# A pooling and mLSTM block on one core: the pooling mixer's group matrices folded into the input projection's weights, the gate applied there too

## The chip, the cores and the metric

The kernel runs on one core of a Trainium2 chip. The metric is device time in microseconds (us) from launch to end; 2048 tokens of 1024 channels go through the block once. Engines are named as in the profile: PE (TensorE), DVE (VectorE), ACT (ScalarE), POOL (GpSimd), and SP (SyncE), which here only issues transfers.

## The reference, cut to what matters

All columns come from one input projection. Branch A pools the u columns over time, multiplies each group of 256 channels by a 256 x 256 matrix, scales each channel and gates it:

```python
h = rms_norm(x, norm_pre_g)
proj = jnp.einsum('bsd,de->bse', h, w_in)              # 1024 -> 9232 columns
u_a, z_a, q, k, v, o, z_b, gates, g_a, g_b = jnp.split(proj, split_points, axis=-1)

pooled = multiscale_pool(u_a)          # group g: mean over a centred window of 2/4/8/16 tokens, minus the token
mixed = jnp.einsum('bsgc,gcd->bsgd', pooled.reshape(B, S, 4, 256), pool_mix_w).reshape(B, S, 1024)
y_a = (mixed * pool_scale) * jax.nn.silu(z_a)
...                                    # branch B: bidirectional mLSTM on q, k, v and the gates -> y_b
p_a = jnp.einsum('bsc,cd->bsd', y_a, w_proj_pool)
p_b = jnp.einsum('bsc,cd->bsd', y_b, w_proj_mlstm)
merged = jax.nn.sigmoid(g_a + b_merge[0]) * p_a + jax.nn.sigmoid(g_b + b_merge[1]) * p_b
out = x + rms_norm(jnp.einsum('bsd,de->bse', merged, w_out), norm_post_g)
```

Pooling acts along the tokens and the group matrix along the channels, so the two commute: pooling `h @ (w_u @ (mix * scale))` gives the same numbers as mixing and scaling the pooled `h @ w_u`.

## The kernel before, in words

**Precision.** A float32 matrix product is done as three products of rounded halves: each operand is split into `hi` (rounded to fp32r, a copy on ACT) and `lo` (the remainder, a subtraction on DVE or POOL; `split`, lines 91 to 98), and PE multiplies hi·hi, hi·lo and lo·hi (`mm3`, lines 106 to 108, with 512 columns; `acc3`, lines 920 to 922, with 256).

**Input projection** (`phase1`). The tokens are taken in two halves of 1024. In each, the columns go by in 36 pairs of 128 + 128 (`in_pairs` writes their order): q, k, v, u, z, o, ga and gb of four heads or groups. A pair is computed by Strassen's scheme in its Winograd form (`strassen`): seven products of 12 matmuls, named by operand (A11·B11, S2·T2, S1·T1, S3·T3, A12·B21, A22·T4, S4·B22), into PSUM banks A, B and C (two buffers each). Bank B is read three times: by the addition to `u2`, by that to `u3` (L395, L400) and at the end. On PE the products of two neighbouring pairs interleave: A11·B11 and S2·T2 of pair i, A22·T4 and S4·B22 of pair i-1, then S1·T1, S3·T3 and A12·B21 of pair i.

In half 0 a pair's weights are loaded (`load_w`, 512 KB at a time), differenced on DVE (L352), split, and the four combinations T1 to T4 kept in memory (`wt{i}`); half 1 loads these back (`again_w`). Columns u are gathered in `raw` and pooled in `pair_u`: doubling sums of windows (the first on POOL, the rest on DVE, L684), the mean minus the token (L688), the few tokens at the edges (L692, L693), then a transfer to `pooled{g}` in memory. Columns z become their SiLU and go to `zs{g}` (`pair_z`). Group g's u pair is number 12, 14, 22, 25 in the order, its z pair 6, 13, 19, 26.

**After it** come the mLSTM (chunks of 128 tokens), branch A, branch B and the output projection, with PE going from one to the next without a barrier. Branch A works on token tiles of 256 (`TT`). For each tile, `mixer` loads the four groups' pooled columns and gates (`xz`), splits the pooled ones (`pxs`), multiplies them by the group's matrix in 48 matmuls (`mps`), scales and gates (L1024), and splits the result (`pys`). `branch_a` multiplies that by w_proj_pool in 192 matmuls per tile (`paps`) and by the sigmoid of g_a. The weights of w_proj_pool are split into 16 blocks (8 row blocks, two column halves): two in `aside` during the mLSTM, four in `then` towards its end, ten once the mLSTM's buffers are free.

**Order.** A scheduler sets each engine's order from the program's order, priorities and its own estimate of times. `tc.issue_after(x)` keeps what is issued within it behind instruction x. Transfers are issued by SP in one list, in order. Pools of a few buffers tie steps together: `acc` (4), `raw` (3) and `p` (6) for the columns, `wraw` (3) and `wc` (20) for weights, `tr` (2) in PSUM for transposes.

Of the kernel before, what the change touches and what calls it, by code (L numbers as in the profile page):

```python
# [13 lines left out]
P = 128  # L14
S = 2048
# [22 lines left out]
LAP = 1  # L38
PB = 2
# [3 lines left out]
PX = "kT"  # L43
# [4 lines left out]
def in_pairs():  # L48
# [11 lines left out]
    light = [("v", 0), ("o", 0), ("z", 0), ("o", 1), ("v", 1), ("o", 2), ("z", 1), ("o", 3), ("v", 2), ("o", 4)]  # L60
    light += [("z", 2), ("o", 5), ("v", 3), ("o", 6), ("z", 3), ("o", 7)]
# [16 lines left out]
class Kernel:  # L78
# [21 lines left out]
    def mm3(self, ps, w, x, start, stop):  # L100

        nc = self.nc
        for kt in range(4):
# [4 lines left out]
            nc.tensor.matmul(ps, wl, xh, start=False, stop=stop and kt == 3, skip_group_check=True)  # L108
# [195 lines left out]
    def load_w(self, wr, i, kts):  # L304
        raw = wr.tile([P, 4, 2 * P], F32, tag="wraw", name=self.nm("wraw"))
        self.nc.sync.dma_start(raw, self.a["w_in"][i, :, kts, :])
        return raw

    def again_w(self, W, i, wr, wc):

        nc, w_in = self.nc, self.a["w_in"]
# [9 lines left out]
        nc.sync.dma_start(left, w_in[i, :, :, :P])  # L321
# [11 lines left out]
        self.read = nc.sync.dma_start(b22, w_in[i, :, 4:8, P:])  # L333
# [35 lines left out]
    def strassen(self, H, W, psum, pool, out, n=BLK, swap=False):  # L369
# [13 lines left out]
        def prod(k, h, w, start):  # L383
            x, y = (H[h], W[w]) if not swap else (W[w], H[h])
            self.mm3(bank[k], y, x, start, True)
# [12 lines left out]
        prod("B", "S3", "T3", False)  # L398
# [38 lines left out]
    def phase1(self):  # L437
        tc, nc, a = self.tc, self.nc, self.a
        with ExitStack() as es:
# [22 lines left out]
            for half in range(2):  # L462
# [49 lines left out]
                rest = iter(())  # L512
                for i in range(2, n):
# [146 lines left out]
    def pair_u(self, half, kind, g, H, W, psum, pool):  # L660
# [6 lines left out]
        for i in range(2):  # L667
# [26 lines left out]
            nc.sync.dma_start(self.sp[f"pooled{g}"][:, i, tstart : tstart + n], d[:, :n])  # L694
# [66 lines left out]
    def spills(self):  # L761
# [4 lines left out]
        for h in range(NH):  # L766
# [4 lines left out]
            for k in ("pooled", "zs", "sga", "sgb"):  # L771
                sp[f"{k}{h}"] = self.dram(f"{k}{h}", [P, 2, S])
# [136 lines left out]
    def late_constants(self):  # L909
        self.cpool = self.ctx.enter_context(self.tc.tile_pool(name="const2", bufs=1, reuse_waits="tile"))  # L910
        self.pscale = self.load("pool_scale", [P, KT])
# [58 lines left out]
    def mix_weights(self, raws, pool):  # L970
        nc = self.nc
        out = []
        for g in range(4):
            raw = raws.tile([P, 2, DH], F32, tag="wraw", name=self.nm("mraw"))
            nc.sync.dma_start(raw, self.a["pool_mix_w"][g])
            out.append(tuple(pool.tile([P, 2, DH], F32R, tag="w", name=self.nm(f"mx{p}")) for p in "hl"))
            self.split(*out[g], raw, "act", "dve")
        return out

# [23 lines left out]
    def mixer(self, t, mix, ya):  # L1003
        nc, sp = self.nc, self.sp
        cut = slice(t * TT, (t + 1) * TT)
        for g in range(4):
            xz = self.pair_of("kT", "xz", F32)
            nc.sync.dma_start(xz[:, 0], sp[f"pooled{g}"][:, :, cut])
            nc.sync.dma_start(xz[:, 1], sp[f"zs{g}"][:, :, cut])
            z = xz[:, 1]  # L1010
            xs = self.pair_of(PX, "pxs")
            self.split(xs[:, 0], xs[:, 1], xz[:, 0], "act", "dve")
            ys = ya[t, g] = self.pair_of("v1h" if g < 2 else "v1l", "pys")
            for i in range(2):
                ps = self.psum.tile([P, 512], F32, tag="t", name=self.nm("mps"), bufs=PB)[:, :TT]
                self.acc3(
                    ps,
                    [
                        (tuple(w[:, kt, i * P : (i + 1) * P] for w in mix[g]), (xs[:, 0, kt, :], xs[:, 1, kt, :]))
                        for kt in range(2)  # L1020
                    ],
                )
                ct = 2 * g + i
                nc.vector.scalar_tensor_tensor(  # L1024
                    z[:, i, :], ps, self.pscale[:, ct : ct + 1], z[:, i, :], op0=ALU.mult, op1=ALU.mult
                )
# [545 lines left out]
```

## Time and profile before

| | |
|---|---|
| median of 3 runs | 2386.11 us (2384.36 to 2393.65) |
| the profiled execution | 2388.18 us, its span 2386.4 us, granted clock 0.993 |
| instructions on PE, DVE, ACT, POOL | 12569, 2495, 1773, 902 |
| half 0, half 1 of the projection | up to 730 us, up to 1440 us |
| mLSTM, branch A, branch B, output | up to 1790.5, 2031.5, 2215 and 2386.4 us |
| matmuls of the mixer (`mps`) | 384 |
| transferred | 521.63 MB, mean 219 GB/s |

The span runs from the first to the last instruction; the execution's own time has little around it. The stages were cut where PE goes from one kind of matmul to the next; neighbours overlap by a few us. A row of the profile that groups instructions gives line, engine, operation, output<-inputs (numbers left out), shape and count; then busy time and mean ns of one; then the idle time before them and what ended it. PE's busy time counts the latency of overlapping matmuls once. A row of a stage gives its bounds and length, the busy time (and instructions) of PE, PEld (weight loads), DVE, ACT and POOL, the granted clock, the DMA engines' busy share, and GB/s.

### The profile page before, as it was taken

The page shows a single profiled execution, that of the slowest core. Times are in us where ns is not written, and L with a number is a line of the kernel's source. Part 1 is how long each engine was busy: PE and PEld are TensorE (multiplying, and loading weights), DVE is VectorE, ACT ScalarE, POOL GpSimd, SP SyncE. Part 2 cuts the span into 40 slices and gives each one's busy share as a digit, 9 for nine tenths or more (in the row PEclk, how much of TensorE's full clock was granted, in tenths as well). Part 3 has the DMA queues.
Part 4 walks back from the last instruction along what each step waited for, and adds up shares of the span by engine and source line. Part 5 has one row for each costly group of instructions (what it writes and reads, how often), then busy time and mean ns, then how long its engine had stood idle before and what let it go on. Part 6 is the DMA issues. An engine that isn't in the chain of part 4 may idle for free.

```text
span 2386.4 us, 35771 instructions
## 1 busy us (share of the span) xinstructions
PE 2313.3 (97%) x12569; PEld 1998.1 (84%) x12569; DVE 1468.2 (62%) x2495; ACT 898.2 (38%) x1773; POOL 1139.3 (48%) x902
## 2 busy tenths in 40 slices
PE   7899999999999989999999999998999999999998
PEld 5688888888887878888888887997989899999776
DVE  6876676677666465565666434887875333354765
ACT  5435333333334333323322234766764112120442
POOL 4655564555544434464564540554555111233775
PEclk9999999999999999999999999999999999999999
DMA  4467656566673566787787867766657546588763
GB/s 151 175 225 273 234 194 238 203 230 215 233 260 135 166 192 216 260 282 256 246 272 239 269 221 253 231 214 208 197 161 230 176 146 208 183 283 280 249 215 124
DMA packets 303011, 521.63 MB, mean 219 GB/s; under 512 B 27504, under 2 KB 138224, under 8 KB 302832
## 3 DMA queue, kind: packets, MB, share of 16 engines
q1 hardware_dynamic: 302832, 519.35, 65.3%
q8 instruction: 99, 1.62, 0.3%
q14 instruction: 80, 0.66, 0.1%
HBM read 318.45 MB, written 200.80 MB: 218 GB/s over the span
## 4 chain that ended last, share of the span: by engine, by line
PE 79%; DVE 8%; DMA 7%; issue 2%; POOL 2%; ACT 2%; SPq 1%; DVEq 0%; POOLq 0%; ACTq 0%
PE bankB L106 8%; PE bankB L107 8%; PE bankB L108 8%; PE bankA L108 5%; PE bankA L107 5%; PE bankC L107 5%; PE bankA L106 5%; PE bankC L106 5%; PE bankC L108 5%; PE num L1212 3%; PE pb L921 2%; PE pb L922 2%; PE pb L920 2%; PE paps L921 2%; PE paps L922 2%
## 5 line engine op out<-in xcount | busy, mean ns | idle before, releaser
L98 POOL TENSOR_TENSOR wB21l<-wraw,wB21h 128x512 fp32r<-128x512 f32 x76 | 107.6, 1416 | 218.9 <-ACT wB21h L94 178.8
L627 DVE SCALAR_TENSOR_TENSOR acc<-raw,conv_w,acc 128x1026 f32<-128x1026 f32 (+1 forms) x96 | 155.8, 1636 | 10.6 <-ACT acc L622 9.7
L1196 POOL TENSOR_TENSOR qs<-q,isc 128x256 f32<-128x256 f32 x120 | 91.6, 766 | 145.3 <-PE num L1212 63.4
L98 POOL TENSOR_TENSOR wB22l<-wraw,wB22h 128x512 fp32r<-128x512 f32 x76 | 116.6, 1535 | 77.8 <-ACT wB22h L94 55.8
L922 PE MATMUL pb<-oxs,w_proj_mlstml 128*128 128x256 f32 x512 | 143.8, 281 | 0.0
L921 PE MATMUL pb<-oxs,w_proj_mlstmh 128*128 128x256 f32 x512 | 143.8, 281 | 0.0
L920 PE MATMUL pb<-oxs,w_proj_mlstmh 128*128 128x256 f32 x512 | 143.5, 280 | 0.0
L921 PE MATMUL paps<-pys,w_proj_poolh 128*128 128x256 f32 x512 | 142.6, 281 | 0.2 <-POOL pys L98 0.2
L920 PE MATMUL paps<-pys,w_proj_poolh 128*128 128x256 f32 x512 | 141.6, 281 | 1.2 <-DVE sga L1049 1.2
L922 PE MATMUL paps<-pys,w_proj_pooll 128*128 128x256 f32 x512 | 141.3, 281 | 0.0
L98 POOL TENSOR_TENSOR wB11l<-wraw,wB11h 128x512 fp32r<-128x512 f32 x72 | 108.9, 1513 | 54.4 <-ACT wB11h L94 53.6
L395 DVE TENSOR_TENSOR u<-bankB,p 128x512 f32<-128x512 f32 x76 | 52.2, 687 | 107.8 <-PE bankB L108 95.1
L106 PE MATMUL bankC<-S1h,wT1h 128*128 128x512 f32 x272 | 106.5, 392 | 3.4 <-ACT sg L738 3.4
L106 PE MATMUL bankB<-S3h,wT3h 128*128 128x512 f32 x272 | 106.3, 391 | 2.3 <-DVE u L395 2.3
L108 PE MATMUL bankB<-S2h,wT2l 128*128 128x512 f32 x272 | 106.3, 391 | 1.2 <-DVE wT2l L98 1.2
L106 PE MATMUL bankA<-A12h,wB21h 128*128 128x512 f32 x272 | 106.8, 393 | 0.5 <-ACT p L389 0.5
L107 PE MATMUL bankB<-S2l,wT2h 128*128 128x512 f32 x272 | 107.0, 393 | 0.0
L106 PE MATMUL bankB<-A22h,wT4h 128*128 128x512 f32 x272 | 105.9, 389 | 0.8 <-DVE u L400 0.8
L108 PE MATMUL bankC<-S1h,wT1l 128*128 128x512 f32 x272 | 106.5, 392 | 0.0
L107 PE MATMUL bankC<-S1l,wT1h 128*128 128x512 f32 x272 | 106.4, 391 | 0.0
L106 PE MATMUL bankB<-S2h,wT2h 128*128 128x512 f32 x272 | 106.2, 391 | 0.0
L107 PE MATMUL bankB<-S3l,wT3h 128*128 128x512 f32 x272 | 106.0, 390 | 0.0
(443 smaller groups left out, 7677.9 us busy)
## 6 DMA issues: line engine op xcount, KB each, us to landing
wraw<-in_w_in SPq DMA_DIRECT2D x110, 512.0 KB, 4.4
wt<-wT2h SPq DMA_DIRECT2D x34, 256.0 KB, 3.8
wt<-wT1h SPq DMA_DIRECT2D x34, 256.0 KB, 4.6
wt<-wT3h SPq DMA_DIRECT2D x34, 256.0 KB, 3.8
wt<-wT2l SPq DMA_DIRECT2D x34, 256.0 KB, 4.8
wt<-wT1l SPq DMA_DIRECT2D x34, 256.0 KB, 4.3
wt<-wT3l SPq DMA_DIRECT2D x34, 256.0 KB, 3.1
wt<-wT4h SPq DMA_DIRECT2D x34, 256.0 KB, 2.0
```

The costliest lines, as they stand in the source:

```text
L98: return eng.tensor_tensor(lo, x, hi.bitcast(F32), op=ALU.subtract)
L106: nc.tensor.matmul(ps, wh, xh, start=start and kt == 0, stop=False, skip_group_check=True)
L107: nc.tensor.matmul(ps, wh, xl, start=False, stop=False, skip_group_check=True)
L108: nc.tensor.matmul(ps, wl, xh, start=False, stop=stop and kt == 3, skip_group_check=True)
L395: self.read_banks.append(nc.vector.tensor_tensor(u2, bank["B"], p1, op=ALU.add))
L627: nc.vector.scalar_tensor_tensor(acc[:, :n], raw[:, tap : tap + n], self.cw[:, ct, tap : tap + 1], acc[:, :n], op0=ALU.mult, op1=ALU.add,)
L920: nc.tensor.matmul(ps, wh, xh, start=i == 0, stop=False)
L921: nc.tensor.matmul(ps, wh, xl, start=False, stop=False)
L922: nc.tensor.matmul(ps, wl, xh, start=False, stop=i == n)
L1196: nc.gpsimd.tensor_tensor(qs[d], q[:, :, ck], isc[:, d, j % 2, None, :].to_broadcast([P, 2, P]), op=ALU.mult)
L1212: nc.tensor.matmul(pn, qs[d][:, kt, :], state[:, kt, :], start=kt == 0, stop=False)
```

## The change

The mixer's matmuls leave the tail. For each group the matrix `pool_mix_w[g]`, its columns multiplied by `pool_scale`, is multiplied into the u columns of `w_in` before they are used:

- **The fold** (`fold`): eight turns (four groups, two halves of the rows), in half 0, at pairs 3, 5, 7, 9, 12, 14, 16 and 18 (`FOLDS`). In the program a turn's loads (matrix `fm`, scale row `sc`, transposed u weights `fw`) stand at the end of the pair before; in SP's list the matrix and the row come beside the stores of the turn before, the u weights a pair ahead. In its pair, POOL scales the matrix (L327), PE does 8 matmuls of 256 columns in plain float32 (`fps`, L334) behind the last matmul of S3·T3 (`self.third`), ACT copies the result out twice (`fo`), and two transfers bring it to `wu{g}` in memory. The u pairs load their weights from there (`columns`).
- **Gate and split** (`pair_u`): the pooled columns are multiplied on DVE (L735) by their gate, loaded back from `zs{g}` into `zu`; ACT copies the rounded half, POOL subtracts, and both halves go to `ya{g}`. For that the z pairs come earlier, now number 6, 8, 13 and 19, and o pairs later.
- **Branch A**: `pooled` loads the finished halves into `pys`, 8 transfers per tile, as many as the mixer had.
- **Weights**: of w_proj_pool's 16 blocks six are split in `aside`, four in `then`, six after the mLSTM. Other weights of the tail take other rooms.

Line numbers of what stays shift: L395, L400, L684, L688 are now L429, L434, L722, L726, and L920 to L922 are L966 to L968.

```diff
+FOLDS = (3, 5, 7, 9, 12, 14, 16, 18)
...
-    light = [("v", 0), ("o", 0), ("z", 0), ("o", 1), ("v", 1), ("o", 2), ("z", 1), ("o", 3), ("v", 2), ("o", 4)]
-    light += [("z", 2), ("o", 5), ("v", 3), ("o", 6), ("z", 3), ("o", 7)]
+    light = [("v", 0), ("o", 0), ("z", 0), ("z", 1), ("v", 1), ("o", 1), ("z", 2), ("o", 2), ("v", 2), ("o", 3)]
+    light += [("z", 3), ("o", 4), ("v", 3), ("o", 5), ("o", 6), ("o", 7)]
...
+    def columns(self, i):
+        kind, g = self.pairs[i][:2]
+        return self.sp[f"wu{g}"] if kind == "u" else self.a["w_in"][i]
+
+    def fold(self, pool, psum):
+        nc, a, tc = self.nc, self.a, self.tc
+        for g in range(4):
+            for half in range(2):
+                room = self.rows.tile([P, HALF], F32, tag="rb", name=self.nm("fm"))
+                m, sc = room[:, : 2 * DH].rearrange("p (c n) -> p c n", c=2), room[:, 2 * DH : 3 * DH]
+                nc.sync.dma_start(m, a["pool_mix_w"][g])
+                nc.sync.dma_start(sc, a["pool_scale"][g * DH : (g + 1) * DH].partition_broadcast(P))
+                w = pool.tile([P, 2, 4 * P], F32, tag="acc", name=self.nm("fw"))
+                nc.sync.dma_start(w, a["w_uT"][g, :, :, half * 4 * P : (half + 1) * 4 * P])
+                yield
+                nc.gpsimd.tensor_tensor(m, m, sc[:, None, :].to_broadcast([P, 2, DH]), op=ALU.mult)
+                for k2 in range(2):
+                    ps = psum.tile([P, 2, DH], F32, tag="tr", name=self.nm("fps"), bufs=2)
+                    for k in range(2):
+                        n0 = (k2 * 2 + k) * P
+                        with tc.issue_after(self.third.ins):
+                            for ct in range(2):
+                                nc.tensor.matmul(
+                                    ps[:, k, :], w[:, ct, n0 : n0 + P], m[:, ct, :], start=ct == 0, stop=ct == 1
+                                )
+                    o = pool.tile([P, 2, DH], F32, tag="p", name=self.nm("fo"))
+                    nc.scalar.activation(o, ps, AF.Copy)
+                    kt = half * 4 + k2 * 2
+                    nc.sync.dma_start(self.sp[f"wu{g}"][:, kt : kt + 2, :], o)
+                yield
...
+                    if half == 0 and i in FOLDS:
+                        next(fold)
                     next(this)
                     rest = this
+                    if half == 0 and i + 1 in FOLDS:
+                        next(fold)
...
-            nc.sync.dma_start(self.sp[f"pooled{g}"][:, i, tstart : tstart + n], d[:, :n])
+            z = pool.tile([P, HALF + 24], F32, tag="acc", name=self.nm("zu"))
+            nc.sync.dma_start(z[:, :n], self.sp[f"zs{g}"][:, i, tstart : tstart + n])
+            nc.vector.tensor_tensor(d[:, :n], d[:, :n], z[:, :n], op=ALU.mult)
+            nc.scalar.activation(z[:, :n].bitcast(F32R), d[:, :n], AF.Copy)
+            nc.gpsimd.tensor_tensor(d[:, :n].bitcast(F32R), d[:, :n], z[:, :n], op=ALU.subtract)
+            for p, y in enumerate((z, d)):
+                nc.sync.dma_start(self.sp[f"ya{g}"][:, p, i, tstart : tstart + n], y[:, :n])
...
-    def mixer(self, t, mix, ya):
...
+    def pooled(self, t, ya):
         for g in range(4):
...
             ys = ya[t, g] = self.pair_of("v1h" if g < 2 else "v1l", "pys")
...
+            for p in range(2):
+                self.nc.sync.dma_start(ys[:, p].bitcast(F32), self.sp[f"ya{g}"][:, p, :, t * TT : (t + 1) * TT])
...
             def aside():
-                mix.extend(self.mix_weights(raws, w1))
-                WA.update(self.weights("w_proj_pool", 0, range(2), raws, w1))
+                WA.update(self.weights("w_proj_pool", 0, range(6), raws, w1))
...
-                WA.update(self.weights("w_proj_pool", 0, range(2, 6), raws, held[0]))
+                WA.update(self.weights("w_proj_pool", 0, range(6, 8), raws, held[0]))
+                WA.update(self.weights("w_proj_pool", 1, range(2), raws, held[0]))
...
-            self.mixer(1, mix, ya)
-            WA.update(self.weights("w_proj_pool", 0, range(6, 8), raws, w2))
-            WA.update(self.weights("w_proj_pool", 1, range(8), raws, w2))
-            self.branch_a(WA, mix, ya)
+            self.pooled(1, ya)
+            WA.update(self.weights("w_proj_pool", 1, range(2, 8), raws, w2))
+            self.branch_a(WA, ya)
...
-        "pool_scale": col(i["pool_scale"][0]),
+        "pool_scale": f(np.asarray(i["pool_scale"])[0]),
+        "w_uT": f(w_in[:, : 4 * DH].T.reshape(4, 2, P, D).transpose(0, 2, 1, 3)),
```

Where instructions stand on an engine before and after, at three places. First PE at pair 3 of half 0, the first turn of the fold, before (each row: line, operation, output<-inputs with their buffer numbers, shape):

```order
L106 MATMUL bankB_1003<-S3h_403,wT3h_974 128x512
L107 MATMUL bankB_1003<-S3l_404,wT3h_974 128x512
L108 MATMUL bankB_1003<-S3h_403,wT3l_975 128x512
L106 MATMUL bankA_1002<-A12h_397,wB21h_978 128x512
L107 MATMUL bankA_1002<-A12l_398,wB21h_978 128x512
```

And the same place after the change:

```order
L106 MATMUL bankB_1012<-S3h_407,wT3h_983 128x512
L107 MATMUL bankB_1012<-S3l_408,wT3h_983 128x512
L108 MATMUL bankB_1012<-S3h_407,wT3l_984 128x512
L334 MATMUL fps_1108<-fm_956,fw_959 128x256 x4
L334 MATMUL fps_1116<-fm_956,fw_959 128x256 x4
L106 MATMUL bankA_1011<-A12h_401,wB21h_987 128x512
L107 MATMUL bankA_1011<-A12l_402,wB21h_987 128x512
```

The turn's eight matmuls stand between the end of S3·T3 and A12·B21, which followed each other before. Second, DVE in half 1 at the widest window (group 3, 16 tokens; `win` are the window sums, `zs` gates, `u` the readings of bank B), before:

```order
L684 TENSOR_TENSOR win_10788<-win_10786 128x1044
L684 TENSOR_TENSOR win_10790<-win_10788 128x1040
L684 TENSOR_TENSOR win_10792<-win_10790 128x1032
L688 SCALAR_TENSOR_TENSOR pooled_10794<-win_10792,raw_10542 128x1032
L719 TENSOR_TENSOR zs_10801<-u_1881_10767,zs_10801 128x512
L719 TENSOR_TENSOR zs_10800<-bankA_10686,zs_10800 128x512
L692 TENSOR_TENSOR pooled_10794<-win_10792,ih_94 128x7
L395 TENSOR_TENSOR u_1919_10902<-bankB_10874,p_1918_10888 128x512
```

The same window after the change (`zu` is the reloaded gate):

```order
L722 TENSOR_TENSOR win_11060<-win_11058 128x1044
L735 TENSOR_TENSOR pooled_11045<-pooled_11045,zu_11049 128x1032
L722 TENSOR_TENSOR win_11062<-win_11060 128x1040
L722 TENSOR_TENSOR win_11064<-win_11062 128x1032
L726 SCALAR_TENSOR_TENSOR pooled_11066<-win_11064,raw_10808 128x1032
L429 TENSOR_TENSOR u_1983_11179<-bankB_11151,p_1982_11165 128x512
```

The gate multiply of the pair's first tile stands among the window sums of its second, ahead of the next reading of bank B; the two multiplies of the z pair that stood there are gone. Third, PE where the mLSTM ends (`num` are its products of scores with values, `mps` the mixer's), before:

```order
L920 MATMUL mps_17475<-pxs_17463,mxh_15179 128x256
L921 MATMUL mps_17475<-pxs_17463,mxh_15179 128x256
L922 MATMUL mps_17475<-pxs_17463,mxl_15180 128x256
L1215 MATMUL num_17560<-v_2960_14925,sd_17418 128x258
L1216 MATMUL num_17560<-v_2961_14926,sd_17418 128x258
L1215 MATMUL num_17566<-v_2960_14925,sd_17418 128x258
L1216 MATMUL num_17566<-v_2961_14926,sd_17418 128x258
```

And after:

```order
L968 MATMUL paps_17936<-pys_17737,w_proj_pooll_15466 128x256
L966 MATMUL paps_17936<-pys_17737,w_proj_poolh_15471 128x256
L1201 MATMUL s_17559<-q_17363,kT_15197 128x128
L1231 MATMUL num_17519<-v_3132_15532,sd_17447 128x258
L1232 MATMUL num_17519<-v_3133_15533,sd_17447 128x258
L1231 MATMUL num_17525<-v_3132_15532,sd_17447 128x258
```

Where the first tile's mixer matmuls stood among the last chunks, there now stand the first products with w_proj_pool.

More of the change, by code (lines that the diff above doesn't have):

```diff
@@ L107, in mm3 @@
             nc.tensor.matmul(ps, wh, xl, start=False, stop=False, skip_group_check=True)
-            nc.tensor.matmul(ps, wl, xh, start=False, stop=stop and kt == 3, skip_group_check=True)
+            end = nc.tensor.matmul(ps, wl, xh, start=False, stop=stop and kt == 3, skip_group_check=True)
+        return end
     def constants(self):
@@ L320, in again_w @@
         left = wr.tile([P, KT, P], F32, tag="wraw", name=self.nm("wraw"))
[L321 removed]
+        nc.sync.dma_start(left, w_in[:, :, :P])
         b22 = wr.tile([P, 4, P], F32, tag="wraw", name=self.nm("wraw"))
@@ L332, in again_w @@
         kept("T4")
-        self.read = nc.sync.dma_start(b22, w_in[i, :, 4:8, P:])
+        self.read = nc.sync.dma_start(b22, w_in[:, 4:8, P:])
         put("B22", b22, "pool")
@@ L384, in prod @@
             x, y = (H[h], W[w]) if not swap else (W[w], H[h])
-            self.mm3(bank[k], y, x, start, True)
+            return self.mm3(bank[k], y, x, start, True)
         prod("A", "A11", "B11", True)
@@ L397, in strassen @@
         prod("C", "S1", "T1", True)
-        prod("B", "S3", "T3", False)
+        self.third = prod("B", "S3", "T3", False)
         u3 = pool.tile([P, n], F32, tag="p", name=self.nm("u3"))
@@ L511, in phase1 @@
                 run(ops)
-                rest = iter(())
+                rest, fold = iter(()), self.fold(pool, psum)
                 for i in range(2, n):
@@ L770, in spills @@
                 sp[f"v{p}{h}"] = self.dram(f"v{p}{h}", [P, NC_, DH + 2])
-            for k in ("pooled", "zs", "sga", "sgb"):
+            sp[f"wu{h}"] = self.dram(f"wu{h}", [P, KT, 2 * P])
+            sp[f"ya{h}"] = self.dram(f"ya{h}", [P, 2, 2, S])
+            for k in ("zs", "sga", "sgb"):
                 sp[f"{k}{h}"] = self.dram(f"{k}{h}", [P, 2, S])
@@ L968, in out_weights @@
             self.split(*o, made[n], "act", "pool" if k % 2 else "dve")
[L970 to L978, printed above, removed]
     def wt(self, W, kt, n0, n=P):
@@ L1000, in slot @@
         return self.kv.tile(shape, dt, tag=f"{tag}{i}", name=self.nm(name), bufs=1), i
-    def mixer(self, t, mix, ya):
-        nc, sp = self.nc, self.sp
-        cut = slice(t * TT, (t + 1) * TT)
+    def pooled(self, t, ya):
         for g in range(4):
[L1007 to L1012, printed above, removed]
-            ys = ya[t, g] = self.pair_of("v1h" if g < 2 else "v1l", "pys")
[L1014 to L1026, printed above, removed]
-            self.split(ys[:, 0], ys[:, 1], z, "act", "pool")
+            ys = ya[t, g] = self.pair_of("v1h" if g < 2 else "v1l", "pys")
+            for p in range(2):
+                self.nc.sync.dma_start(ys[:, p].bitcast(F32), self.sp[f"ya{g}"][:, p, :, t * TT : (t + 1) * TT])
     def project(self, W, d, X, name):
@@ L1052, in branch_a @@
                 if d == 1 and t + 2 < n:
-                    self.mixer(t + 2, mix, ya)
+                    self.pooled(t + 2, ya)
     def mlstm(self, aside=None, then=None, last=None):
```

18 lines of the change are left out of this document (8 added, 10 removed).

## The prediction

> **What bounds the kernel now.** I read the page's first two parts, then the same engines stage by stage, then TensorE's own instructions and its waits. The page first:
>
> ```profile
> PE 2313.3 (97%) x12569; PEld 1998.1 (84%) x12569; DVE 1468.2 (62%) x2495; ACT 898.2 (38%) x1773; POOL 1139.3 (48%) x902
> ...
> PEclk9999999999999999999999999999999999999999
> ```
>
> TensorE (PE) is busy 97% of the span at full granted clock, and no other engine reaches two thirds. The stages (stretch, length, then each engine's busy time with its instructions, granted clock, DMA share, GB/s):
>
> ```profile
> 110.00:730.00 620.00, 619.81 (x2774) 513.84 (x2773) 420.06 (x500) 235.06 (x389) 335.64 (x218) 1.00 0.65 231
> ...
> 850.00:1440.00 590.00, 584.09 (x2603) 483.81 (x2601) 319.82 (x391) 181.53 (x269) 288.48 (x194) 1.00 0.76 247
> 1440.00:1790.50 350.50, 331.27 (x2188) 303.55 (x2187) 275.01 (x909) 228.14 (x659) 158.94 (x201) 0.99 0.67 211
> 1790.50:2031.50 241.00, 231.80 (x1937) 229.21 (x1937) 96.40 (x192) 63.46 (x108) 61.38 (x47) 1.00 0.59 188
> 2031.50:2215.00 183.50, 183.50 (x1548) 183.09 (x1547) 86.67 (x142) 29.35 (x48) 61.87 (x72) 1.00 0.75 253
> ```
>
> They are the two halves of the input projection, the mLSTM, branch A and branch B. In the halves and in branch B PE never rests. In the mLSTM it rests 19 us and VectorE (DVE) is busy 275 of 350. In branch A it rests 9 us. So a matmul taken out of branch A is worth its pace, a matmul put into a half costs its pace, and other engines' work costs only where PE has to wait for it.
>
> The busy time of one matmul is its latency, so I price by pace. Branch B shows it: 183.50 us for 1548 matmuls of 256 columns is 118 ns each.
>
> **Removed: the mixer's matmuls.** By form (instructions; busy us and mean ns of one; idle before):
>
> ```profile
> L921 PE MATMUL mps<-pxs,mxh 128*128 128x256 f32 x128 | 35.8, 282 | 0.7 <-DVE pxs L98 0.7
> L920 PE MATMUL mps<-pxs,mxh 128*128 128x256 f32 x128 | 35.5, 289 | 7.0 <-ACT pxs L94 5.5 <-DVE gb L1266 1.2 <-DVE xz L1024 0.3
> L922 PE MATMUL mps<-pxs,mxl 128*128 128x256 f32 x128 | 35.5, 280 | 0.0
> ```
>
> There are 384 of them (8 token tiles, 4 groups, 2 column halves, 2 row blocks, 3 products), all inside branch A's stretch: 384 x 118 ns = **45.3 us off**. At that pace the stretch's 1937 matmuls need 228.6 of its 241.0 us; 12.4 us are waits, and 7.7 of them stand in the rows above (the mixer waiting for its own ScalarE and DVE splits). Those 7.7 go with it. The rest stays: after the mLSTM the second column half of w_proj_pool still has to be loaded and split, though six blocks of it now and no longer eight, with two more blocks of the first half done earlier.
>
> The order shows a further gain: the first paps matmuls now stand among the mLSTM's last chunks, because their operand only needs a load. They can fill PE's pauses there; the mLSTM's longest wait in the whole run's list of waits is this (total, times, longest):
>
> ```profile
> PE num L1212 <- ACT h L1245: 8.4, 7, 2.4
> ```
>
> About 80 paps stand ahead of the last num, 9.4 us of work. I book **4 us** of it as filling, near the middle: nothing if the chunks' own pace is held up by it, 9.4 if all falls into pauses. Branch A and the end of the mLSTM together: 45.3 + 7.7 + 4 = **57.0 us off**.
>
> **Added: the fold on PE.** Eight turns, each with 8 matmuls of 256 columns in plain float32, all in the first half, where PE has no idle time: 64 in all. Their nearest kin is the float32 product of the scaled query with the state, 258 columns. Of it the profile keeps two records per matmul (120 matmuls, 240 records). Its pace, from the timeline (start, us, engine, line, records):
>
> ```profile
> 1784.78 1.03 PE L1212 MATMUL num<-cb,qs 128*128 128x258 f32 x4
> 1785.46 0.47 PE L1215 MATMUL num<-v,sd 128*128 128x258 f32 x1
> 1785.77 0.28 PE L1216 MATMUL num<-v,sd 128*128 128x258 f32 x1
> 1785.89 0.28 PE L1217 MATMUL num<-v,sd 128*128 128x258 f32 x1
> ```
>
> From 1784.78 to 1785.77 ran two float32 matmuls and one of the 0.12 us kind: (0.99 - 0.12) / 2 = 0.435 us, 0.43 for 256 columns. 64 x 0.43 = **27.6 us on**. The other price would be that of a rounded product, 0.118 us, 7.6 us in all; the operands here are plain float32, so I take the upper end.
>
> **The fold on the other engines.** ScalarE copies 16 times 512 elements out of PSUM at 0.58 us, POOL scales 8 times at 1.4 us, and SP issues 40 transfers (24 in, 16 out, 11 MB). I cost them at nothing, since a turn has long cover: its inputs are requested right after the turn before it, one or two pairs earlier, and a pair lasts 7 x 12 matmuls x 0.227 us = 19 us. A load lands in 4.4 us (below), so the cover fails only beyond some 13 us. The pooled pairs read the folded weights two pairs or more after they are written. The first turn's scaling on POOL stands ahead of the splits of S1 at the start, where POOL was idle 3 us; 0 to 3 us, I take **1**.
>
> ```profile
> 62.42 6.74 POOL L98 TENSOR_TENSOR S1l<-xT,S1h 128x512 fp32r<-128x512 f32 x4 [3.10 <-ACT S1h L94]
> ...
> wraw<-in_w_in SPq DMA_DIRECT2D x110, 512.0 KB, 4.4
> ```
>
> **Moved: gating and splitting of the pooled columns.** Per pooled tile of 1016 or 1032 columns (16: 4 pairs, 2 tiles, 2 halves): a reload of the gate, one DVE multiply, one ScalarE copy, one POOL subtraction, two transfers out where there was one. Nearest rows (ns min/median/max; the last line is the gate's transfer, us):
>
> ```profile
> L684 DVE TENSOR_TENSOR win<-win x24: 1204/1542/2331, 349.5 to 1295.1; 128x1016 f32<-128x1016 f32 x6, 128x1032 f32<-128x1032 f32 x6, 128x1020 f32<-128x1020 f32 x2, 128x1028 f32<-128x1028 f32 x2
> L758 POOL TENSOR_TENSOR gB<-gB,gB x16: 2396/2406/3401, 178.0 to 1340.8; 128x1024 f32<-128x1024 f32 x16
> L395 DVE TENSOR_TENSOR u<-bankB,p x76: 674/691/694, 100.5 to 2366.3; 128x512 f32<-128x512 f32 x76
> DMA to landing us min/median/max: 2.6/3.8/6.9
> ```
>
> That is 25 us on DVE, 38 on POOL, 17 on ScalarE and 32 more SP issues over 1200 us in which they are busy 62, 53, 35%: no engine fills up. What counts is the queue. A multiply that waits for its gate, or lasts 2.3 us, holds up DVE's next reading of bank B (L395), which PE needs before its third product may add to that bank. Between lie the previous pair's last two products and S1 T1, 3 x 2.72 us, so 7.5 us of delay are free. The one place in the halves where this reserve ran out is the widest window in the second half:
>
> ```profile
> 1297.37 1.24 DVE L688 SCALAR_TENSOR_TENSOR pooled<-win,raw 128x1032 f32<-128x1032 f32 x1
> ...
> 1299.79 0.68 DVE L395 TENSOR_TENSOR u<-bankB,p 128x512 f32<-128x512 f32 x1
> ...
> 1300.53 0.50 PE L106 MATMUL bankB<-S3h,wT3h 128*128 128x512 f32 x1 [0.59 <-DVE u L395]
> ```
>
> PE waited 0.6 us there, and DVE was behind by three window adds. One multiply now stands among them, while two gate multiplies (the z pair was moved away) have left. I take **3 us** for all eight pairs: 0 if the reserve holds, 16 x 0.8 = 13 us if every tile costs a third of the longest row. The kept weights are reloaded nine products ahead, so the denser DMA of the second half (share 0.76; 8 MB more) has 20 us of cover.
>
> What is removed from DVE, ScalarE and POOL in branch A was not on the path, apart from the waits above. Pooling loads stay as many (64 of 256 KB), so branch A's DMA, share 0.59, carries the same bytes in 4/5 of the time, as branch B did at 0.75.
>
> **Sum.** -57.0 + 27.6 + 1 + 3 = **-25.4 us**. The profiled span of 2386.4 becomes 2361.0; that execution took 2388.18 us and the median is 2386.11, as near as its span, so I forecast 2361.
>
> **A rule against it.** The float32 rows of DVE show a second value: among the weight differences, all of one shape,
>
> ```profile
> L352 DVE TENSOR_TENSOR wt<-wraw,wraw x34: 674/1760/2392, 60.4 to 701.9; 128x512 f32<-128x512 f32 x34
> ```
>
> take 0.67 or 1.76 us, while L395, which reads one operand from PSUM, never leaves 0.69. The Trainium skill (SBUF — State Buffer, section "Who interferes with whom") explains it: a DVE instruction with two SBUF inputs and a GpSimd instruction that reads SBUF exclude each other for the whole instruction. The rows agree. By it the 24 added POOL instructions could each stop DVE for their full length, 16 x 2.41 + 8 x 1.4 = 50 us; DVE idles 38% of the halves, so the sum would move only through rival 2.
>
> **Rivals.** (1) PE rests after the mLSTM after all: the paps that fill pauses are taken from what covered the late weight blocks, so nothing is filled, and the 12.4 us of waits stay. Then -45.3 + 27.6 + 4 = -13.7, **2372**; with the stall bounds above, 2376. For it: the blocks are still split only when the mLSTM's buffers are free. Against: less is left to split.
> (2) The other side: **slower**. Each of the 16 multiplies waits for its reloaded gate with the bank readings behind it. Landing spreads from 2.6 to 6.9 us, so 4.3 us apiece at most, 69 us: 2361 - 3 + 69 = **2427**. It makes the kernel slower by over 0.5% from (25.4 + 3 + 11.9) / 16 = 2.5 us per tile. Against: the reserve of 7.5 us, and that the gate is requested before the pooled tile is finished. For: SP issues in order and its list now holds waits on ScalarE and POOL between weight loads.
> (3) The fold's turns stall PE: each waits for its scaled matrix or its PSUM buffer. At 3 us in 8 turns, +24: **2385**, no change. Against: the 19 us of cover.
> (4) It goes better: all 9.4 us of paps fall into pauses, the other 4.7 us of branch A's waits vanish, and no stall appears: -45.3 - 12.4 - 9.4 + 27.6 = -39.5, **2346.5**.
>
> **How the numbers follow.** A measurement of this kernel can tell about 0.5% (12 us) from no change: faster is below 2374, slower above 2398. The forecast (2353 to 2369 by its own bounds) has 0.60, rival 4's side 0.14, rival 1 0.12 (half of it below 2374), rival 3 0.07, rival 2 0.07. Faster 0.60 + 0.14 + 0.06 = 0.80, same 0.06 + 0.07 = 0.13, slower 0.07. The range runs from rival 4 to the worse end of rival 1 with a few us of rival 3: 2346 to 2380, leaving out rival 2, most of rival 3 and a little at the lower end, under 0.2.
>
> **What would show it.** The fold's records: 128, with 3.4 us per turn from its first to the next product. Branch A about 57 us shorter from the first num pause to the first pb, no mps, PE idle there under 7 us. The first half longer by 28 to 31 us, the second by 0 to 5. I am wrong if PE's waits name DVE u L429 or vtr often, if a turn is preceded by idle PE, or if the first paps wait for weights.

## The result, and the profile after

The changed kernel takes 2409.73 us (median of 5 runs, 2401.73 to 2413.04); the kernel before, on the same chip, 2386.11. The ratio is 1.0092, interval 1.0078 to 1.0105: slower by 22 us, where 25 us less was forecast. The profiled execution took 2411.85 us, its span 2410.1. The page:

```profile
PE 2312.6 (96%) x12313; PEld 1987.4 (82%) x12313; DVE 1460.1 (61%) x2411; ACT 877.9 (36%) x1737; POOL 1161.6 (48%) x894
```

PE has 256 instructions fewer and is busy as long as before (2313.3). The stages after (columns as in the prediction's rows), cut where the same kind of matmul starts as before:

```profile
110.00:778.10 668.10, 655.33 (x2915) 541.44 (x2914) 438.37 (x508) 250.74 (x415) 369.90 (x233) 0.99 0.69 244
778.10:1503.10 725.00, 709.74 (x3125) 581.54 (x3124) 417.60 (x507) 232.73 (x352) 369.88 (x238) 0.99 0.72 236
1503.10:1868.70 365.60, 341.85 (x2246) 315.21 (x2246) 276.47 (x908) 227.87 (x660) 161.53 (x204) 0.97 0.70 221
1868.70:2054.50 185.80, 181.14 (x1494) 180.51 (x1494) 44.83 (x93) 22.12 (x39) 17.27 (x13) 0.97 0.62 202
```

Half 0 grew from 620 to 668 us, half 1 from 710 to 725, the mLSTM from 350.5 to 365.6; branch A fell from 241 to 186. So +48.1, +15.0, +15.1, -55.2, and 0.7 behind: 23.7. Where PE waited (total, times, longest), after:

```profile
PE num L1228 <- ACT h L1261: 14.7, 6, 3.5
PE bankB L106 <- DVE u L434: 11.1, 7, 4.0
PE bankB L106 <- DVE u L429: 8.6, 4, 4.3
PE vtr L691 <- DVE raw L632: 6.8, 5, 2.2
PE paps L966 <- DMA pys<-ya: 4.3, 2, 2.7
```

The same two readings of bank B before:

```profile
PE bankB L106 <- DVE u L395: 5.5, 3, 3.2
PE bankB L106 <- DVE u L400: 1.8, 3, 0.8
```

They rose from 7.3 us to 19.7 over the whole span. In the projection alone (110 us to the first score matmul) they were these, before and then after:

```profile
PE bankB L106 <- DVE u L400: 0.8, 1, 0.8
PE bankB L106 <- DVE u L395: 0.6, 1, 0.6
```
```profile
PE bankB L106 <- DVE u L434: 8.4, 4, 4.0
PE bankB L106 <- DVE u L429: 4.6, 2, 4.3
```

Beside them the waits of `vtr` for `raw` rose from 1.2 us to 6.8, and those for `pys` are new. The fold is as priced: one turn in the timeline (start, us) and the group,

```profile
166.71 0.39 PE L108 MATMUL bankB<-S3h,wT3l 128*128 128x512 f32 x1
166.94 3.62 PE L334 MATMUL fps<-fm,fw 128*128 128x256 f32 x16
170.20 0.58 PE L106 MATMUL bankA<-A12h,wB21h 128*128 128x512 f32 x1
```
```profile
L334 PE MATMUL fps<-fm,fw 128*128 128x256 f32 x128 | 29.1, 380 | 1.6 <-DMA fw<-in_w_uT 1.6
```

show 16 records in 3.3 us, 128 in all. Each turn moved PE's next pair by 3.5 us, 28 us together.

In what follows "halves" is the start of the first score matmul (`s<-q,kT`, before at 1486.0), "mLSTM" goes from there to the last `num` matmul (1793.5), "A" from there to the first `pb` (2031.5). All medians are compared with runs of the kernel before on the same chip.

| run | median us | ratio to before (interval) | halves | mLSTM | A |
|---|---|---|---|---|---|
| before | 2386.11 | | | 307.5 | 238.0 |
| changed | 2409.73 | 1.0092 (1.0078 to 1.0105) | +63.1 | 322.6 | 182.7 |
| e1 gate in the tail | 2396.87 | 1.0043 (1.0032 to 1.0055) | +28.3 | 340.0 | 183.8 |
| e2 no fold | 2363.83 | 0.9907 (0.9892 to 0.9922) | +29.1 | 311.9 | 180.9 |
| e3 tail only | 2339.06 | 0.9805 (0.9791 to 0.9820) | -0.3 | 314.1 | 180.0 |
| e4 subtraction on DVE | 2396.12 | 1.0049 (1.0033 to 1.0066) | +49.8 | 320.8 | 182.3 |
| e5 no gate | 2388.04 | 1.0006 (0.9994 to 1.0017) | +45.8 | 315.4 | 180.5 |
| e6 gate in the tail, PE tied | 2393.64 | 1.0034 (1.0020 to 1.0048) | +32.9 | 334.4 | 185.8 |
| e7 changed, PE tied | 2405.14 | 1.0080 (1.0060 to 1.0099) | +65.0 | 313.0 | 182.2 |
| e8 gate in the tail, all tied | 2380.13 | 0.9972 (0.9960 to 0.9985) | +32.6 | 306.6 | 194.5 |
| e9 e8, turns moved | 2381.90 | 0.9986 (0.9977 to 0.9995) | +34.6 | 310.1 | 193.0 |
| e10 e8, multiply in the halves | 2383.53 | 0.9998 (0.9987 to 1.0008) | +37.2 | 312.8 | 189.8 |
| e11 gate requested earlier | 2406.18 | 1.0081 (1.0058 to 1.0104) | +62.7 | 320.8 | 180.2 |
| e12 e11 and e4 | 2399.25 | 1.0066 (1.0051 to 1.0081) | +57.4 | 321.1 | 180.3 |
| e13 hi over raw | 2399.34 | 1.0054 (1.0036 to 1.0071) | +60.2 | 317.1 | 181.9 |
| e14 e13 and e4 | 2390.00 | 1.0012 (1.0002 to 1.0021) | +44.6 | 318.6 | 182.7 |

One of e4's four executions took 3270.31 us at a granted clock of 0.655, and its median here is that of the other three.

The last three columns come from one profiled execution each, and they scatter. e1, e6 and e8 have the same code in the projection and put the halves at +28.3, +32.9 and +32.6; the changed kernel and e7 share theirs too, +63.1 and +65.0. In the seven runs whose order on PE and ACT is the same behind the halves (changed, e4, e5, e11 to e14) mLSTM and A together took from 495.9 to 505.3 us. So a difference of under 5 us in the halves, or under 10 us behind them, is not shown by one pair of runs.

### The profile page after: what moved, and what is told of

Same layout as the page of the kernel before. It is cut to its first block, busy times and chain, and to the rows that moved or that the text cites. A ratio compares the mean times of both kernels' runs of the same rounds, so it can differ in the third digit from the quotient of the medians.

```text
span 2410.1 us, 35162 instructions
## 1 busy us (share of the span) xinstructions
PE 2312.6 (96%) x12313; PEld 1987.4 (82%) x12313; DVE 1460.1 (61%) x2411; ACT 877.9 (36%) x1737; POOL 1161.6 (48%) x894
## 5 line engine op out<-in xcount | busy, mean ns | idle before, releaser
L966 PE MATMUL paps<-pys,w_proj_poolh 128*128 128x256 f32 x512 | 145.7, 285 | 4.3 <-DMA pys<-ya 4.3
L967 PE MATMUL paps<-pys,w_proj_poolh 128*128 128x256 f32 x512 | 145.3, 285 | 0.3 <-DMA pys<-ya 0.3
L966 PE MATMUL pb<-oxs,w_proj_mlstmh 128*128 128x256 f32 x512 | 143.8, 281 | 1.2 <-DVE sgb L1360 1.2
L968 PE MATMUL paps<-pys,w_proj_pooll 128*128 128x256 f32 x512 | 144.0, 284 | 0.0
L968 PE MATMUL pb<-oxs,w_proj_mlstml 128*128 128x256 f32 x512 | 143.3, 280 | 0.0
L429 DVE TENSOR_TENSOR u<-bankB,p 128x512 f32<-128x512 f32 x76 | 52.1, 686 | 101.4 <-PE bankB L108 93.8
L106 PE MATMUL bankC<-S4h,wB22h 128*128 128x512 f32 x272 | 106.3, 391 | 2.4 <-DVE u L749 2.4
L108 PE MATMUL bankB<-S3h,wT3l 128*128 128x512 f32 x272 | 107.7, 396 | 0.0
L108 PE MATMUL bankB<-A22h,wT4l 128*128 128x512 f32 x272 | 107.4, 395 | 0.0
L107 PE MATMUL bankB<-A22l,wT4h 128*128 128x512 f32 x272 | 107.3, 395 | 0.0
```

Source lines behind the costliest of these rows:

```text
L106: nc.tensor.matmul(ps, wh, xh, start=start and kt == 0, stop=False, skip_group_check=True)
L107: nc.tensor.matmul(ps, wh, xl, start=False, stop=False, skip_group_check=True)
L108: end = nc.tensor.matmul(ps, wl, xh, start=False, stop=stop and kt == 3, skip_group_check=True)
L429: self.read_banks.append(nc.vector.tensor_tensor(u2, bank["B"], p1, op=ALU.add))
L966: nc.tensor.matmul(ps, wh, xh, start=i == 0, stop=False)
L967: nc.tensor.matmul(ps, wh, xl, start=False, stop=False)
```

## The experiments

### Which part of the change costs: e1, e2, e3

e1 puts gate and split back into branch A; the u pairs store the pooled columns as they are:

```diff
...
+            nc.vector.tensor_tensor(z, xz[:, 0], z, op=ALU.mult)
+            self.split(ys[:, 0], ys[:, 1], z, "act", "pool")
```

> The changed kernel with the gate multiply and the split of the pooled columns put back into branch A (loads of pooled columns and gates, one multiply on DVE, copy on ACT, subtraction on POOL per group and tile); the fold, the pair order and the weights stay. Theory A (the moved gating and splitting make PE wait in the halves): half 0 is longer than before by 28 to 33 us instead of 47.7, half 1 by 0 to 4 instead of 14.8, branch A loses at most some us more, and the median is 2378 to 2390. Rival B (the fold, its traffic and the new pair order make PE wait): the halves stay some 62 us longer, and the median is 2405 or more.

Measured: the halves are 28.3 us longer than before, so theory A holds there: the moved gating and splitting cost 35 us in the halves, or 30 by e6 and e8, which have the same projection. The median did not come down as far, because the mLSTM took 340.0 us (e6 and e8).

e2:

```diff
-FOLDS = (3, 5, 7, 9, 12, 14, 16, 18)
+FOLDS = ()
...
-        return self.sp[f"wu{g}"] if kind == "u" else self.a["w_in"][i]
+        return self.a["w_in"][i]
```

> The changed kernel without the fold: the u pairs load their weights from w_in, so group matrix and scale are left out of the result; gating, splitting, order and tail stay. Theory A: the fold costs its 27.6 us on PE and the 2 to 4 us that its matmuls waited for their loads, so the median is 2376 to 2383, and the waits around the u pairs stay in both halves (half 0 longer than before by 15 to 20 us). Rival B (the fold's POOL work and traffic cause the other waits too): half 0 comes back to within 5 us of before and the median is below 2370.

Measured: 46 us less than the changed kernel, more than A, and a median on rival B's side. But the halves lost only 34 us (28 of matmuls, the other 6 little more than the scatter), and half 0 is still 14.3 us longer than before. So the waits around the u pairs stay without the fold: B's cause falls. The last 12 us came from the mLSTM and branch A, whose code is the same. How much of that is the fold's is open, since the two together differ by up to 9.4 us among runs with one order there.

e3 adds to e2 the pair order of before, and in `pair_u`:

```diff
-            z = pool.tile([P, HALF + 24], F32, tag="acc", name=self.nm("zu"))
...
-            for p, y in enumerate((z, d)):
-                nc.sync.dma_start(self.sp[f"ya{g}"][:, p, i, tstart : tstart + n], y[:, :n])
+            for p in range(2):
+                nc.sync.dma_start(self.sp[f"ya{g}"][:, p, i, tstart : tstart + n], d[:, :n])
```

> Only the tail of the change: no fold, no gating and no split in the projection (pooled columns are stored twice as they are, so mix, scale and gate are left out), pair order as before; branch A loads finished halves and its weights as in the changed kernel. Prediction's terms: 45.3 + 7.7 + 4 us less, a median of 2329. Theory A (the new loads make PE wait in their turn, and the mLSTM gains nothing): about 40 us less, 2346. Rival (the tail is worth only the matmuls and all the rest was in the halves): 45.3 us less, 2341.

Measured: 45.1 us less than before (43 to 50 by the interval), nearest to the rival, which has the matmuls alone. The halves are as before. In the profiled executions the mLSTM and branch A were together 51.4 us shorter. So of the 11.7 us of mixer waits and filling about 6 may have been gained, or nothing; this run does not settle it.

### Why the halves lose: e4, e5, e10

The places where PE waited show DVE late. One of them, at the end of pair 15 in half 0 of the changed kernel (DVE, then POOL):

```profile
387.35 1.70 DVE L735 TENSOR_TENSOR pooled<-pooled,zu 128x1016 f32<-128x1016 f32 x1
388.97 1.78 DVE L386 TENSOR_TENSOR wt<-wraw,wraw 128x512 f32<-128x512 f32 x1
390.68 3.38 DVE L726 SCALAR_TENSOR_TENSOR pooled<-win,raw 128x1016 f32<-128x1016 f32 x1
393.98 0.68 DVE L749 TENSOR_TENSOR u<-bankC,u 128x512 f32<-128x512 f32 x1
```
```profile
390.22 2.77 POOL L737 TENSOR_TENSOR pooled<-pooled,zu 128x1016 fp32r<-128x1016 f32 x1
```

L726 needs 1.20 us alone. Here it ended 3.38 us after its start, 1.1 us after POOL's subtraction (L737), which had begun before it: it ran only when POOL was done. PE waited 2.4 us for the reading of bank C behind it. e4 moves that subtraction:

```diff
-            nc.gpsimd.tensor_tensor(d[:, :n].bitcast(F32R), d[:, :n], z[:, :n], op=ALU.subtract)
+            nc.vector.tensor_tensor(d[:, :n].bitcast(F32R), d[:, :n], z[:, :n], op=ALU.subtract)
```

> The changed kernel with the 16 subtractions of the split in the u pairs moved from POOL (2.5 us each) to DVE (1.23 us each). Theory lock (DVE is late because each long POOL instruction stops its two-operand instructions): the stretched DVE instructions beside the u pairs go back from 1.7 to 3.4 us to 1.2 or less, and the kernel gets faster by 5 to 12 us, 2398 to 2405. Rival queue (DVE is late because it has more work in a fixed order ahead of the bank readings): 20 us more on DVE, slower by 4 to 15 us, 2414 to 2425.

Measured: the halves got 13 us shorter although DVE had 16 instructions of together 25.6 us more to do. The page of e4:

```profile
PE 2304.4 (96%) x12313; PEld 1980.7 (83%) x12313; DVE 1465.5 (61%) x2427; ACT 876.5 (37%) x1737; POOL 1126.2 (47%) x878
```

DVE's busy time rose by 5.4 us only, from 1460.1, so its other instructions got 20 us shorter. L726 in the changed kernel, then in e4 (ns min/median/max):

```profile
L726 DVE SCALAR_TENSOR_TENSOR pooled<-win,raw x16: 1201/1448/3376, 334.8 to 1358.8; 128x1016 f32<-128x1016 f32 x8, 128x1032 f32<-128x1032 f32 x8
```
```profile
L726 DVE SCALAR_TENSOR_TENSOR pooled<-win,raw x16: 1203/1232/2319, 332.5 to 1348.3; 128x1016 f32<-128x1016 f32 x8, 128x1032 f32<-128x1032 f32 x8
```

The longest went from 3.38 to 2.32 us; other work on POOL stays. That DVE merely has too much to do is refuted. POOL also had 35.4 us less to do; no run separates what that alone did for the halves. The Trainium skill (SBUF — State Buffer, section "Who interferes with whom") has the rule, whoever starts first keeps the shared read interface for the whole instruction; these rows agree.

e5 leaves out the gate:

```diff
-            nc.sync.dma_start(z[:, :n], self.sp[f"zs{g}"][:, i, tstart : tstart + n])
-            nc.vector.tensor_tensor(d[:, :n], d[:, :n], z[:, :n], op=ALU.mult)
```

> The changed kernel without the gate in the u pairs: no reload of z and no multiply on DVE (the gate is left out of the result); ACT copy, POOL subtraction and the two stores stay. With the subtraction on DVE the two halves together were 49.6 us longer than before, in the changed kernel 62.5. Theory A (multiplies and gate waits carry what the subtraction on POOL does not): the halves are 40 to 50 us longer than before, the median 2387 to 2398. Rival B (the POOL instructions carry it all by stopping DVE): the halves stay 56 to 62 us longer, the median is 2403 or more. If both are needed together, the halves fall to 35 or less.

e10 takes e8 (below) and puts reload and multiply back into the u pairs; copy and subtraction stay in branch A:

```diff
+            nc.sync.dma_start(z[:, :n], self.sp[f"zs{g}"][:, i, tstart : tstart + n])
+            nc.vector.tensor_tensor(d[:, :n], d[:, :n], z[:, :n], op=ALU.mult)
             nc.sync.dma_start(self.sp[f"pooled{g}"][:, i, tstart : tstart + n], d[:, :n])
```

> The gate multiply stays in the u pairs (reload of z, DVE multiply, one store), copy and subtraction of the split go to branch A, tied behind the mLSTM as in the two runs above. Theory A (multiply and POOL subtraction cost PE much only together, the one lengthening DVE's list, the other stopping it): the halves are 32 to 40 us longer than before. Rival B (the multiplies and their waits for the gate carry the stall by themselves): 44 us or more. With a quiet mLSTM the median is 2370 to 2385 by A, 2385 or more by B.

Measured: +45.8 without the multiply, +37.2 with the multiply alone, +32.6 with neither (e8). So copy and POOL subtraction alone cost 13 us, the multiply alone 5 (no more than the scatter), both 30: they cost most together. Theory A holds in both runs; e10's median is that of before.

### Gate and slots: e11 to e14

The prediction had the gate requested before the pooled tile is finished. It is not: the gate's tile takes the `acc` slot that the last window frees. Half 1 of the changed kernel, DVE and SP:

```profile
1289.95 2.26 DVE L730 TENSOR_TENSOR pooled<-win,ih 128x3 f32<-128x3 f32 x1
...
1296.98 1.23 DVE L735 TENSOR_TENSOR pooled<-pooled,zu 128x1032 f32<-128x1032 f32 x1 [3.15 <-DMA zu<-zs]
```
```profile
1292.24 0.32 SPq L734 DMA_DIRECT2D zu<-zs  x1
```

SP issued the reload the moment L730 ended (1292.2). L730 had taken 2.26 us, not 0.15; a subtraction on POOL (L737, 1288.79 to 1292.19) ended just before it. DVE then waited. Over the run, DVE waited for gates 16.1 us in 7 waits. e11 takes the gate's tile and requests it ahead of the last window sum; e12 does that with the subtraction on DVE:

```diff
+                if 2 * step == w:
+                    z = pool.tile([P, HALF + 24], F32, tag="acc", name=self.nm("zu"))
+                    nc.sync.dma_start(z[:, :n], self.sp[f"zs{g}"][:, i, tstart : tstart + n])
                 d = pool.tile([P, HALF + 24], F32, tag="acc", name=self.nm("win"))
...
```

> The changed kernel with the gate's tile taken and its reload requested ahead of the last window sum of each pooled tile, not behind the finished tile. In the changed kernel the reload waits in SP's list for the slot that the last window frees, and DVE then waits 16.1 us in all for gates. Theory A (the late request is a cause): DVE waits for gates under 7 us in all, the two halves are 50 to 57 us longer than before instead of 62.5, the median is 2395 to 2405. Rival B (the slot is only missed elsewhere, by a window or a gate): the halves stay at 59 to 66 us, the median at 2405 or more.

> The early request of the gate and the subtraction on DVE together. Theory A (both causes add): with the subtraction on DVE alone the halves were 49.6 us longer than before; now 38 to 46, and the median is 2383 to 2394. Rival B (what is left with the subtraction on DVE is DVE's longer list, not the gates): the halves stay at 47 to 53 us, the median at 2395 or more.

Measured: rival B in e11. There the waits for gates fell to 4.8 us, and waits for slots came up in their place (DVE's waits):

```profile
DVE win L725 <- DMA ya<-zu: 14.1, 4, 6.4
DVE pooled L729 <- DMA ya<-zu: 7.3, 1, 7.3
DVE pooled L736 <- DMA zu<-zs: 4.8, 2, 2.8
```

e12 came out worse than e4 (+57.4 to +49.8), beyond the range of either side; why is open. e13 frees a slot: `hi` is written over the raw columns; e14 adds e4:

```diff
-            nc.scalar.activation(z[:, :n].bitcast(F32R), d[:, :n], AF.Copy)
+            nc.scalar.activation(raw[:, :n].bitcast(F32R), d[:, :n], AF.Copy)
...
```

> The changed kernel with the rounded half of the gated columns written over the raw u columns, which are no longer needed, and not over the gate, so that the gate's slot among the four is free after the multiply and not after the store. Theory A (the shortage of slots, which a gate requested earlier only moved to the windows, is what makes DVE late): DVE's waits for gates and slots fall from 25 us to under 12, the halves are 45 to 56 us longer than before instead of 62.5, the median is 2390 to 2403. Rival B (the slots are a symptom; DVE's instructions stopped by POOL decide): the halves stay at 59 to 65 us.

> The same with the subtraction on DVE. Theory A (slots and stopped DVE instructions are separate causes): the halves are 36 to 45 us longer than before (with the subtraction on DVE alone 49.6), the median is 2382 to 2394. Rival B (they are one cause, since a stopped DVE is what holds the slots): 46 to 53 us, no better than the subtraction on DVE alone.

Measured: in e13 DVE waited 14.1 us for gates and for buffers held by stores of gated columns, instead of 24.6. Of these, 5.0 us are a new wait for a `raw` buffer, which now is held until its store has landed. The halves moved by 2.9 us only: rival B. Its median is 10 us lower, mostly from the tail. In e14 the halves came to +44.6, 5 us under e4 and within A. So a slot freed earlier is worth some 3 us with the subtraction on POOL and 5 without it, at the edge of the scatter: at most the smaller cause.

### The tail: e7, e6, e8, e9

e7 ties the first tile's `paps` on PE behind the last `num` (`self.final`):

```diff
...
-                ps = self.project(W, d, [ya[t, g] for g in range(4)], "paps")
+                with self.tc.issue_after(self.final.ins) if t == 0 else ExitStack():
+                    ps = self.project(W, d, [ya[t, g] for g in range(4)], "paps")
```

> The changed kernel with the same tie alone: no matmul with w_proj_pool ahead of the mLSTM's last. The prediction booked 4 us of such matmuls as filling pauses, so by it the kernel gets slower by 4 us (2414). Theory A (they fill nothing, their 9.4 us only stand elsewhere): no change, 2406 to 2413, the mLSTM shorter by about 9 us and branch A longer by as much. Rival B (they hold up the chunks behind them): faster by 5 to 10 us, 2399 to 2405.

Measured: not slower; the median is 4.6 us lower, with intervals that overlap, at the border of A and B. The mLSTM got 9.6 us shorter than in the changed kernel (2 to 8 us shorter than in the six other runs with that order), and branch A no longer, though it has 79 matmuls more. After the early start it had waited for its next `pys` (4.3 us above) at a granted clock of 0.97; in e7 PE is busy for all of its 182.2 us at 1.00. So no gain from the paps in the mLSTM is seen.

e6 is e1 with that tie; e8 also queues the first two tiles' multiply and splits behind the mLSTM's last DVE, ACT and POOL instructions (`self.ends`), and the first tile's loads stand behind the mLSTM in the program, no longer within it:

```diff
...
+                for i in self.ends if t < 2 else ():
+                    es.enter_context(self.tc.issue_after(i.ins))
                 nc.vector.tensor_tensor(z, xz[:, 0], z, op=ALU.mult)
                 self.split(ys[:, 0], ys[:, 1], z, "act", "pool")
```

> Gate and split in branch A (as in the run with the gate in the tail), and the first token tile's matmuls with w_proj_pool are issued on PE behind the mLSTM's last matmul, not among its chunks. Theory A (in that run the mLSTM was 32.5 us longer than before because 80 such matmuls stood in PE's order waiting for splits that ACT and POOL made late): the mLSTM comes back to within 8 us of before, last mLSTM matmul to first branch B matmul takes 188 to 196 us (before 238), the halves stay 28 to 32 us longer, and the median is 2362 to 2374, below the kernel before. Rival B (the splits themselves slow the mLSTM down): the mLSTM stays 15 us or more longer and the median is 2380 or more.

> As the tied run with the gate in the tail, but gate multiply and splits of the first two token tiles are also queued behind the mLSTM's last instructions on DVE, ACT and POOL (loads as early as they can). Theory A (in that run DVE waited up to 5.9 us for the gates' loads with the mLSTM's chain queued behind it): the mLSTM takes 300 to 316 us (before 307.5, there 334.4), last mLSTM matmul to first branch B matmul takes 188 to 200 us, and the median is 2366 to 2380, below the kernel before. Rival B (the mLSTM is slow because its order was made anew, whatever stands beside it): the mLSTM stays at 325 us or more, and the median is 2386 or more.

Measured: e6 stayed at 334.4 us in the mLSTM, rival B. DVE waited there for gates in 8 waits, 17.6 us in all, the longest 5.9. Its rows ahead of PE's longest pause, then PE:

```profile
1815.77 0.93 DVE L1041 TENSOR_TENSOR xz<-xz 128x512 f32<-128x512 f32 x1 [1.95 <-DMA xz<-zs]
1816.63 1.75 DVE L98 TENSOR_TENSOR w_proj_pooll<-wraw,w_proj_poolh 128x512 fp32r<-128x512 f32 x1
1818.30 0.27 DVE L1258 TENSOR_TENSOR r<-r,num 128x1 f32<-128x1 f32 x3
```
```profile
1820.42 2.08 PE L1228 MATMUL num<-cb,qs 128*128 128x258 f32 x4 [6.44 <-ACT h L1261]
```

DVE stood for a gate's load, then did the multiply and a weight split, with the mLSTM's own steps (`r`, from which ACT makes `h`) queued behind them. In e8, where none of these gate waits falls in the mLSTM, it took 306.6 us, theory A. With 2380.13 us e8 is a little under both kernels: 0.28% under before (interval 0.15 to 0.40%), 1.2% under the changed one. Branch A takes 12 us more than in e7: the first splits now stand between it and the mLSTM (3.8 us of waits for `pys`), and its granted clock was 0.97, not 1.00.

e9 is e8 with other turns:

```diff
-FOLDS = (3, 5, 7, 9, 12, 14, 16, 18)
+FOLDS = (4, 5, 7, 10, 13, 15, 17, 19)
```

> As the run before it, with the fold's turns at pairs 4, 5, 7, 10, 13, 15, 17 and 19. Theory A (the 1.6 us at pair 3 and some 2 us at pair 9 come from turns that share POOL with the start's splits and with the statistics of the second half): half 0 is longer than before the change by 27 to 29 us instead of 31 to 35, and the kernel 2 to 5 us faster than the run before it. Rival B (any pair with a turn makes PE wait about as often): no difference within 2 us.

Measured: rival B, no gain. The wait at pair 3 went, the one at pair 9 grew from 4.1 to 7.1 us, though no turn stands there now: it does not come from a turn in that pair. e2, without any turn, has none there.

## Why the prediction was wrong

- **Removed matmuls, 45.3 us: borne out as far as e3 tells** (45.1 by the medians, 51.4 by the profiled stages); it holds these matmuls, waits and filling in one.
- **Mixer waits, 7.7 us, and filling, 4 us: wrong in the changed kernel.** mLSTM and branch A together gained 40.2 us, not 57.0 (42.4 to 49.6 in the six other runs with that order). Branch A's 1457 remaining paps need 171.9 us at 118 ns and took 182.7: PE's waits, above all for `pys` (4.7 us idle in all), and half speed (10.2 us, before none) stand where the mixer's waits were. The mLSTM grew by 15.1 us. Its 79 paps, less 18 mixer matmuls that had stood there, account for 7.2; half speed lasted 23.9 us there, before 10.2. The step that failed was to count a wait as gone with the instruction at which it stood. Besides, 1.2 of the 7.7 us ended with `gb` of the mLSTM and not with a split of the mixer.
- **Fold, 27.6 us: right** (28 us; 1.6 us of waits for `fw`). The start cost 1 us, as booked; with it pairs 3 and 9 lost 1.6 and 2 us, which e2 did not.
- **Gating and splitting, 3 us, bound 13: the main miss.** They cost 30 to 35 us (+63.1 in the halves against +32.6 and +28.3 in e8 and e1). The step was "7.5 us of delay are free", with DVE's durations taken from rows of before. In its place the runs showed DVE late beyond that reserve: PE's idle time in the halves rose from 9.6 us to 30.6, with the waits that the prediction itself had named as signs of being wrong, for `u` and at `vtr`. The added POOL subtractions, up to 3.40 us each, stop DVE instructions in a row (e4: 13 us). That a multiply, a late gate and stretched window sums add up with them past the reserve fits e5 and e10, but no run shows the sum pair by pair. The same rule was weighed under "A rule against it" and put aside because DVE idles 38%: a share of the stage, where the stall is made in one pair. Rival 2 was the right side, though its cause, waits for gates, is the smaller one (e11, e13).
- **Readings and sums.** PE "never rests" in the halves is not what the rows say: in half 1 it was busy 584.09 of 590.00 us, with one wait of 5.3 us at `vtr`. Rival 1 with the stall bounds of 3 and 13 us comes to 2384, not 2376, so the upper end of the range, built on it, was too low. The terms' own bounds give 2352 to 2377, not 2353 to 2369. None of these reaches 2409.73.
- **What was not in the sum at all: the clock** (below). In the halves half speed lasted 20.5 us, before 3.4; at half speed that is 8.5 us more lost, at most that much of the 30.

## What to carry to other kernels

Work moved to engines that are half idle is not free when the bounding engine waits for them in a fixed order: cost it at the pair where the queue is longest, with the durations it will have beside the other engine's long instructions. A wait is gained only if what is late next is named; here one was traded for another three times (mixer for `pys`, gate for slot, chunk for split). Once PE is full, look at what a pause costs after it has ended.

## What the runs showed that was not expected

A pause of PE costs more than its length. The longest in half 0, in the timeline, and the stretches around it:

```profile
653.81 0.39 PE L108 MATMUL bankB<-S2h,wT2l 128*128 128x512 f32 x1
658.23 0.79 PE L106 MATMUL bankB<-A22h,wT4h 128*128 128x512 f32 x1 [4.03 <-DVE u L434]
658.82 0.63 PE L107 MATMUL bankB<-A22l,wT4h 128*128 128x512 f32 x1
659.25 0.63 PE L108 MATMUL bankB<-A22h,wT4l 128*128 128x512 f32 x1
659.67 0.63 PE L106 MATMUL bankB<-A22h,wT4h 128*128 128x512 f32 x1
```
```profile
653.40:656.10 2.70, 0.80 (x4) 0.34 (x2) 2.70 (x2) 0.00 (x0) 2.44 (x2) 1.00 0.25 97
656.10:662.90 6.80, 4.67 (x11) 3.70 (x12) 5.87 (x6) 4.10 (x7) 4.04 (x3) 0.53 0.35 126
```

After a wait of 4.0 us the matmuls start 0.43 us apart, not 0.227, and the granted clock is 0.53: what follows came some 6.7 us late: 4.2 by the pause, and half of the 5.1 us that the half speed still lasted. The clock records of the 16 traces show half speed in stretches of 3.41 us or a multiple, but for those that the end of a trace cuts off. For each idle time of PE behind 110 us one can see whether such a stretch began within it or up to 3.5 us after it: so it was in 43 of 46 that lasted 3.4 us or more, in 85 of 112 between 2 and 3.4 us, in 19 of 146 between 1 and 2. The Trainium skill (TensorE: Matmul & The Clock Gate, section "Part 1: The HAM clock gate (the "warmup" mystery)") has half rate after an idle window of about 3.4 us; the length agrees, but here pauses well under it were followed by half speed as well. The mean granted clock fell from 0.993 to 0.985: (1 - 0.985) x 2410.1 - (1 - 0.993) x 2386.4 = 19 us more of the span without clock, at most that much of the miss of 49 (some of it falls where PE waits anyway).
